# Attention mask as extra features, output weights cast later, channel sum on VectorE, three products moved forward

## The chip, the cores and the metric

The kernel runs on one core of a Trainium2 chip. The metric is the device time of one execution in microseconds (us). A difference of about 0.2% (3.6 us) is what a measurement of this kernel can tell from none.

## The reference

Two layers of a Conformer block on 512 tokens of width 1024. Each layer is a half-weighted SwiGLU, a mixing stage, a second half-weighted SwiGLU and a norm. The mixing stage, where the change lies, is this:

```python
h = rms_norm(x, mix_norm);  p = h @ w_in
# group A: 8 heads, q and k of 96 features (64 + 32 rotary), v of 64
scores = q @ k.T * 96 ** -0.5                  # keys up to the end of the 128-row query tile
allowed = k_chunk <= q_chunk                   # chunks of 64 tokens
scores = where(allowed, scores, -1e30)
attn = softmax(scores) @ v
# group B: conv module on 512 channels
u = a * sigmoid(g)
y = causal_depthwise_conv(u, 31 taps) + conv_b
conv = silu(layer_norm(y, ln_g, ln_b))         # mean and variance over the 512 channels
x = x + concat(attn, conv) @ w_out
```

## The kernel before

Activations lie as features (128 partitions) by tokens (512 columns). Every large product in float32 precision is done as three float32r products (`mm3`, lines 151 to 155): high by high, high by low, low by high. A weight block of 128x1024 is loaded by SP, cast to the high part on ScalarE (ACT, line 136), and its low part is made either by a subtraction on VectorE (DVE) or GpSimd (POOL) (line 142), or, for the kind "sum", by ACT writing the negated block (line 139) and a POOL-queued DMA that adds the weight to it in memory (line 140). The pools hold 3 raw blocks, 4 high and 4 low parts.

The program is written in order, and a scheduler sets the order of each engine's queue; `issue_after(i)` keeps what stands in it behind instruction i in that order. Each engine then works its own queue in order.

The mixing stage (`mix_body`) first makes the projections, the queries `q` and keys `kn` (tokens by heads by 96 features). Then, for eight heads, with a lag of some steps between them: `turn` transposes a head's queries and keys (TensorE, PE, lines 765 and 770; evicted by ACT at 767 and DVE at 772); `scores` makes four score blocks of 128, 256, 384 and 512 keys (788), adds the mask with a small bf16 product into the last 64 columns of each (789: a row of ones for the first 64 queries by a row of -1e30), takes the maximum on DVE (790) and the exponential with its row sum on ACT (794); `turn_p` transposes the probabilities (809, evicted by DVE, ACT, DVE at 812); `values` multiplies by v (822) and, for each pair of heads, normalises on DVE (829); `turn_out` transposes the result of a pair (840) and splits it into high and low parts (159, 160), which gives one of the four blocks `at`.

The depthwise convolution runs beside this. Channel blocks 0 and 3 are done on DVE (876), each ended by a copy on ACT (886). Blocks 1 and 2 are done by ACT and POOL together: per tap, ACT writes the scaled shifted input `pr` (880, three buffers) and POOL adds it (884). The last 15 adds of block 1 and all 30 of block 2 are held behind the last inverse norm of the keys.

After that comes the layer norm over channels: POOL sums the four blocks (898 to 900), PE spreads the mean with a matrix of 1/512 (902), DVE subtracts it (908), ACT squares and DVE adds (185, 189), PE sums over channels (196), POOL takes the inverse root (171), PE spreads it (215), DVE scales (918), ACT applies SiLU (920), and the split gives the four blocks `cv`. The output projection multiplies eight blocks of output weights `wo` by `at` and `cv`. The products with `at` of the first weight blocks fill PE while the layer norm's chain runs; they stand behind the last score product. The first four `wo` blocks are loaded and cast as soon as the keys are done (line 866), with kind "sum"; the others come late, with the subtraction on POOL.

## Time and profile before

| | us |
|---|---|
| median of 3 runs | 1815.6 |
| lowest, highest | 1813.96, 1816.92 |
| the profiled execution, its own time | 1814.81 |
| span of its profile, first to last instruction | 1813.0 |
| idle time of PE within the span (1813.0 - 1791.5) | 21.5 |
| first to last exponential, layer 0 | 463.4 to 508.1 |
| first to last exponential, layer 1 | 1356.0 to 1400.7 |

The profile gives, for each engine, the time it was busy and what it waited for; a row of the timeline has the start, the length, the engine, the line, the operation, out<-in, and in brackets the idle time before it with what ended it. Rows of the same kind that follow each other are merged (xN), and then the length runs from the first start to the last end. The length of a row includes the end of an instruction that overlaps the next one's start, so the distance between starts is what one more instruction costs. A float32 product shows two records for each instruction.

### The profile page before, as it was taken

The page shows a single profiled execution, that of the slowest core. Times are in us where ns is not written, and L with a number is a line of the kernel's source. Part 1 is how long each engine was busy: PE and PEld are TensorE (multiplying, and loading weights), DVE is VectorE, ACT ScalarE, POOL GpSimd, SP SyncE. Part 2 cuts the span into 40 slices and gives each one's busy share as a digit, 9 for nine tenths or more (in the row PEclk, how much of TensorE's full clock was granted, in tenths as well). Part 3 has the DMA queues.
Part 4 walks back from the last instruction along what each step waited for, and adds up shares of the span by engine and source line. Part 5 has one row for each costly group of instructions (what it writes and reads, how often), then busy time and mean ns, then how long its engine had stood idle before and what let it go on. Part 6 is the DMA issues. An engine that isn't in the chain of part 4 may idle for free.

```text
span 1813.0 us, 30598 instructions
## 1 busy us (share of the span) xinstructions
PE 1791.5 (99%) x12198; PEld 1649.3 (91%) x12198; DVE 1423.0 (78%) x1975; ACT 1089.3 (60%) x1685; POOL 422.7 (23%) x343
## 2 busy tenths in 40 slices
PE   9899999999999999999999999999999999999998
PEld 7799999888788899999888999998978788999997
DVE  5988887679965978887679888865999568888873
ACT  4565656447953565656645656564679435656564
POOL 1000000238944001010220000002589420000001
PEclk9999999999999999999999999999999999999999
DMA  5466665323203456565325575743250125565642
GB/s 177 115 166 159 156 158 129 127 76 113 63 1 112 121 154 166 150 165 141 111 76 160 126 189 126 189 117 110 80 143 9 36 87 157 142 183 132 183 115 73
DMA packets 70415, 226.23 MB, mean 125 GB/s; under 512 B 7936, under 2 KB 8320, under 8 KB 70272
## 3 DMA queue, kind: packets, MB, share of 16 engines
q1 hardware_dynamic: 54000, 169.74, 27.8%
q0 software_dynamic: 16128, 54.53, 17.5%
q8 instruction: 95, 1.56, 0.3%
q14 instruction: 48, 0.39, 0.1%
q10 hardware_dynamic: 144, 0.00, 0.0%
HBM read 222.15 MB, written 2.10 MB: 124 GB/s over the span
## 4 chain that ended last, share of the span: by engine, by line
PE 80%; DVE 9%; ACT 5%; POOL 3%; issue 2%; DMA 0%; ACTq 0%; POOLq 0%; DVEq 0%
PE ps L154 25%; PE ps L152 25%; PE ps L153 25%; POOL y L884 2%; PE ps L822 1%; ACT pr L880 1%; DVE wl L244 1%; DVE r L160 1%; DVE x L449 1%; ACT r L794 1%; PE ps L788 1%; DVE cv L876 1%; DVE wl L142 1%; DVE r L311 1%; PE ps L196 0%
## 5 line engine op out<-in xcount | busy, mean ns | idle before, releaser
L152 PE MATMUL ps<-r,wh 128*128 128x256 f32 (+1 forms) x3436 | 1062.3, 312 | 5.7 <-ACT r L159 5.0
L153 PE MATMUL ps<-r,wh 128*128 128x256 f32 (+1 forms) x3436 | 1063.9, 310 | 0.0
L154 PE MATMUL ps<-r,wl 128*128 128x256 f32 (+1 forms) x2668 | 846.8, 319 | 2.2 <-DVE wl L142 0.8
L152 PEld LDWEIGHTS ps<-r,wh 128*128 128x128 f32 x3436 | 652.1, 190 | 45.4 <-ACT r L159 6.7
L153 PEld LDWEIGHTS ps<-r,wh 128*128 128x128 f32 x3436 | 653.6, 190 | 36.6 <-issue 2.4
L154 PEld LDWEIGHTS ps<-r,wl 128*128 128x128 f32 x2668 | 507.7, 190 | 40.4 <-DVE wl L244 2.6
L136 ACT CAST wh<-raw 128x1024 fp32r<-128x1024 f32 (+3 forms) x148 | 132.1, 900 | 221.1 <-PE ps L153 102.8
L367 POOL DMA_DIRECT2D ls<-in_wgu x72 | 62.7, 871 | 744.3 <-ACT ls L366 617.6
L142 DVE TENSOR_TENSOR wl<-raw,wh 128x1024 fp32r<-128x1024 f32 (+3 forms) x132 | 146.4, 1115 | 100.1 <-ACT wh L136 93.2
L242 ACT CAST wh<-fr 128x1024 fp32r<-128x1024 f32 (+1 forms) x160 | 157.6, 985 | 101.2 <-DVE fr L387 43.5
L154 PE MATMUL ps<-r,ls 128*128 128x256 f32 x768 | 216.7, 282 | 0.0
L244 DVE TENSOR_TENSOR wl<-fr,wh 128x1024 fp32r<-128x1024 f32 (+1 forms) x160 | 182.3, 1139 | 39.5 <-ACT wh L242 39.5
L884 POOL TENSOR_TENSOR y<-y,pr 128x511 f32<-128x511 f32 (+14 forms) x120 | 157.6, 1314 | 54.6 <-ACT pr L880 47.3
L154 PEld LDWEIGHTS ps<-r,ls 128*128 128x128 f32 x768 | 145.2, 189 | 0.0
L244 DVE TENSOR_TENSOR wl<-raw,wh 128x1024 fp32r<-128x1024 f32 (+1 forms) x100 | 113.3, 1133 | 24.7 <-ACT wh L242 24.2
L189 POOL TENSOR_TENSOR r<-r,t 128x512 f32<-128x512 f32 x45 | 77.4, 1729 | 172.6 <-ACT t L185 171.8
L242 ACT CAST wh<-raw 128x1024 fp32r<-128x1024 f32 (+1 forms) x100 | 97.9, 979 | 27.9 <-PE ps L153 20.0
L366 ACT ACTIVATE ls<-fr 128x1024 fp32r<-128x1024 f32 (+1 forms) x56 | 56.1, 1002 | 78.6 <-PE ps L154 66.6
L880 ACT ACTIVATE pr<-r,vec 128x511 f32<-128x511 f32 (+14 forms) x120 | 85.5, 737 | 10.2 <-POOL y L884 10.2
L876 DVE SCALAR_TENSOR_TENSOR cv<-r,vec,cv 128x511 f32<-128x511 f32 (+14 forms) x120 | 87.7, 731 | 3.4 <-ACT cv L872 2.1
L449 DVE SCALAR_TENSOR_TENSOR x<-ps,x 128x512 f32<-128x512 f32 x112 | 77.0, 688 | 16.5 <-PE ps L154 16.1
L367 POOL DMA_DIRECT2D ls<-in_wdq x32 | 27.7, 865 | 260.1 <-ACT ls L366 260.1
(220 smaller groups left out, 2439.0 us busy)
## 6 DMA issues: line engine op xcount, KB each, us to landing
fr<-in_wgu SPq DMA_DIRECT2D x112, 512.0 KB, 3.7
ls<-in_wgu POOLq DMA_DIRECT2D x72, 512.0 KB, 6.4
raw<-in_wgu SPq DMA_DIRECT2D x62, 512.0 KB, 5.1
fr<-in_wdq SPq DMA_DIRECT2D x48, 384.0 KB, 4.6
ls<-in_wdq POOLq DMA_DIRECT2D x32, 384.0 KB, 4.7
raw<-in_wd SPq DMA_DIRECT2D x32, 384.0 KB, 3.1
raw<-in_wd SPq DMA_DIRECT2D x32, 256.0 KB, 2.7
raw<-in_wcv SPq DMA_DIRECT2D x16, 512.0 KB, 3.2
```

The lines of the kernel that those rows point to most:

```text
L136: order["cast"] = A.copy(hi[:, :w], raw[:, :w]).ins
L142: (G if kind in POOLW.split() else V).tensor_tensor(lo[:, :w], raw[:, :w], hi[:, :w].bitcast(FP), ALU.subtract)
L152: T.matmul(o, lh, rh, start=first, stop=False, skip_group_check=free)
L153: T.matmul(o, lh, rl, start=False, stop=False, skip_group_check=free)
L154: order["mm"] = T.matmul(o, ll, rh, start=False, stop=last, skip_group_check=free).ins
L242: A.copy(hi[:, :w], src[:, :w])
L244: order["lo"] = V.tensor_tensor(lo[:, :w], src[:, :w], hi[:, :w].bitcast(FP), ALU.subtract).ins
L367: G.dma_start(out=lo[:, :n], in_=w, accum_op=ALU.add)
L449: return V.scalar_tensor_tensor(v, o.rearrange("p (m t) -> p m t", m=2), 0.5 * sign, v, ALU.mult, ALU.add).ins
L876: V.scalar_tensor_tensor(acc[:, s:], u[c][:, :S - s], tap(k), acc[:, s:], ALU.mult, ALU.add)
L880: A.activation(pr[:, s:], u[c][:, :S - s], AF.Copy, scale=tap(k))
L884: order["conv"] = G.tensor_tensor(acc[:, s:], acc[:, s:], pr[:, s:], ALU.add).ins
```

## The change

- Mask: `q` and `kn` get 100 columns per head, not 96. Column 96+t of a query is 1 for the first 64 tokens of token tile t, and of a key is -1e30 for the last 64 tokens of tile t. They come from the constants (32 columns more) by two POOL products per layer (`mask_columns`). Transposes, evictions and score products take 100 rows; the 64 mask products (32 per layer) and their constants are gone.
- Output weights: only three blocks are loaded with kind "sum", and each is put behind the last exponential of head 0, 2 and 4. The fourth is now of the kind with the subtraction on POOL.
- Products: the nine products of the first output block with the first three blocks of `at` are put right behind the last `values`, ahead of the last `turn_out`.
- Channel sum: three adds on DVE in place of three on POOL, with the last POOL block added last; the mean's matrix is all ones, and the scale -1/512 moves into the subtraction on DVE.

```diff
+DM = DQ + 4
-EARLY = "s"
+WOH = (0, 2, 4)
-WOP = 4
-CN = 256
+CCOS, CSIN, CID, CMQ, CMK = 0, 64, 128, 256, 272
+CN = 288
...
-        q = kpool.tile([P, NT, H, DQ], FP, tag="q", name=nm("q"), bufs=1)
-        kn = kpool.tile([P, NT, H, DQ], FP, tag="kn", name=nm("kn"), bufs=1)
+        q = kpool.tile([P, NT, H, DM], FP, tag="q", name=nm("q"), bufs=1)
+        kn = kpool.tile([P, NT, H, DM], FP, tag="kn", name=nm("kn"), bufs=1)
...
+        def mask_columns(v, o):
+            G.tensor_tensor(v[:, :, :, DQ:DM], cst[:, o:o + 16].rearrange("p (t i) -> p t i", t=NT)[:, :, None, :]
+                            .to_broadcast([P, NT, H, 4]), ones.rearrange("p (t h i) -> p t h i", t=NT, h=H), ALU.mult)
...
-                T.matmul(o, qT[0:DQ, i * P:(i + 1) * P], kT[0:DQ, 0:n], start=True, stop=False)
-                heads[h]["s"] = T.matmul(o[:, n - 64:n], mrow, mneg, start=False, stop=True).ins
+                heads[h]["s"] = T.matmul(o, qT[0:DM, i * P:(i + 1) * P], kT[0:DM, 0:n], start=True, stop=True).ins
...
+        wo, early = [], []
+        def early_products(ms, ks):
+            for m in ms:
+                if m == len(early):
+                    early.append(bank())
+                group(early[m], wo[m], at, ks, KD)
         for step in range(H + 6):
             for stage, lag in STAGES:
                 h = step - lag
+                if stage is turn_out and h == H - 1:
+                    for m, i in enumerate(WOH):
+                        with tc.issue_after(order["keys"]), tc.issue_after(heads[i]["e"]):
+                            wo.append(load_w(wout[l, m], WC, "sum"))
+                    with tc.issue_after(order["values"]):
+                        early_products((0,), range(3))
...
-        with tc.issue_after(order["keys"]):
-            wo = [load_w(wout[l, m], WC, "sum") for m in range(WOP)]
...
+        with tc.issue_after(heads[H - 1]["s"]):
+            early_products((0,), range(3, 4))
         ysum = tmp()
-        G.tensor_tensor(ysum, ys[0], ys[1], ALU.add)
-        G.tensor_tensor(ysum, ysum, ys[2], ALU.add)
-        (G if YP else V).tensor_tensor(ysum, ysum, ys[3], ALU.add)
+        for a, b in ((ys[0], ys[1]), (ysum, ys[3]), (ysum, ys[2])):
+            V.tensor_tensor(ysum, a, b, ALU.add)
         pm = bank()
-        T.matmul(pm, onesm, ysum, start=True, stop=True)
+        T.matmul(pm, ones, ysum, start=True, stop=True)
...
-            V.tensor_tensor(ys[c], ys[c], pm, ALU.subtract)
+            V.scalar_tensor_tensor(ys[c], pm, -1.0 / CW, ys[c], ALU.mult, ALU.add)
...
+    consts[:64, CMQ:CMQ + 16] = np.eye(NT, dtype=f32).reshape(-1)
+    consts[64:, CMK:CMK + 16] = f32(-1e30) * np.eye(NT, dtype=f32).reshape(-1)
```

How the queues move. First ACT's queue in layer 0 from the first exponential of head 0 (r,sums is the exponential with its row sum, pr a conv tap, wh and wl the two parts of an output weight block). Before, the fourth weight block stands just ahead of it:

```order
L880 ACTIVATE pr_5573<-r_4161,vec 128x488
L880 ACTIVATE pr_5576<-r_4161,vec 128x487
L139 ACTIVATE wl_5467<-raw_5463 128x1024
L136 CAST wh_5465<-raw_5463 128x1024
L880 ACTIVATE pr_5579<-r_4161,vec 128x486
L794 ACTIVATE r_4887,sums_4885<-ps_4882,mx_4886 128x128
L880 ACTIVATE pr_5582<-r_4161,vec 128x485
```

In the change (the exponential is at line 787 there, the tap at 885, the cast at 123 and the negated copy at 126) taps stand ahead of it, and the first weight block comes behind the last exponential of head 0:

```order
L885 ACTIVATE pr_5550<-r_4153,vec 128x484
L885 ACTIVATE pr_5553<-r_4153,vec 128x483
L787 ACTIVATE r_4881,sums_4879<-ps_4876,mx_4880 128x128
L787 ACTIVATE r_4882,sums_4879<-ps_4877,mx_4880 128x384
L885 ACTIVATE pr_5556<-r_4153,vec 128x482
L787 ACTIVATE r_4883,sums_4879<-ps_4878,mx_4880 128x512
L761 ACTIVATE r_4901<-ps_4896,gqs_4802 100x512
L123 CAST wh_5397<-raw_5395 128x1024
L787 ACTIVATE r_4914,sums_4879<-ps_4910,mx_4913 128x128
L126 ACTIVATE wl_5399<-raw_5395 128x1024
```

So three weight blocks that stood ahead of the first exponential in the queue, and the fourth just ahead of it, now stand between exponentials. From the first exponential to the last (the 256-wide one of head 7) ACT's queue has 79 rows before in either layer: 32 exponentials, 32 taps, 15 evictions and copies. In the change it has 85 in layer 0 and 83 in layer 1: 31 and 29 taps, and 7 rows of output weights.

The third and the fourth block, further on in ACT's queue of the change, stand behind the last exponential of head 4 (to `sums_5062`) and ahead of the eviction of transposed probabilities (line 805):

```order
L885 ACTIVATE pr_5605<-r_4730,vec 128x496
L787 ACTIVATE r_5066,sums_5062<-ps_5061,mx_5063 128x512
L123 CAST wh_5411<-raw_5409 128x1024
L126 ACTIVATE wl_5413<-raw_5409 128x1024
L123 CAST wh_5844<-raw_5842 128x1024
L805 COPY r_5087<-ps_5086 128x512
L885 ACTIVATE pr_5608<-r_4730,vec 128x495
```

No such rows stand there before; there the eviction follows the exponential.

Last, the end of the attention stage on PE (layer 0). Before, the last transposes (840) and the mean's product (902) follow the last values (822):

```order
L822 MATMUL ps_5399<-r_4880,r_5388 128x64
L840 MATMUL ps_5433<-cst,t_5431 128x128 x4
L902 MATMUL ps_5722<-t_5718,onesm 128x512
L152 MATMUL ps_5726<-r_5210,wh_5444 128x512
L153 MATMUL ps_5726<-r_5211,wh_5444 128x512
L154 MATMUL ps_5726<-r_5210,wl_5446 128x512
```

In the change nine products with weights (139 to 141) stand between:

```order
L815 MATMUL ps_5361<-r_4874,r_5350 128x64
L139 MATMUL ps_5416<-r_5180,wh_5397 128x512
L140 MATMUL ps_5416<-r_5181,wh_5397 128x512
L141 MATMUL ps_5416<-r_5180,wl_5399 128x512
L139 MATMUL ps_5416<-r_5305,wh_5397 128x512
L140 MATMUL ps_5416<-r_5306,wh_5397 128x512
L141 MATMUL ps_5416<-r_5305,wl_5399 128x512
L139 MATMUL ps_5416<-r_5377,wh_5397 128x512
L140 MATMUL ps_5416<-r_5378,wh_5397 128x512
L141 MATMUL ps_5416<-r_5377,wl_5399 128x512
L833 MATMUL ps_5426<-cst,t_5393 128x128 x4
L899 MATMUL ps_5690<-t_5686,ones 128x512
```

Between the mean's product and the product that sums the squares stand 24 products of this kind before and 15 in the change; further on the counts are the same. On DVE the three adds of the channel sum stand behind the normalisation of the last pair of heads (829), ahead of the last split.

## The prediction

> **What bounds the kernel now.** I read the page's busy times first:

> ```profile
> span 1813.0 us, 30598 instructions
> ...
> PE 1791.5 (99%) x12198; PEld 1649.3 (91%) x12198; DVE 1423.0 (78%) x1975; ACT 1089.3 (60%) x1685; POOL 422.7 (23%) x343
> ```

> PE looks like the bound everywhere, ACT nowhere. But the change lies in one stage per layer, so the windows come next, split at the first score product and the last exponentials (columns: the stretch, its length, then busy time and count of PE, PEld, DVE, ACT, POOL, granted clock, DMA):

> ```profile
> core 0: us, PE busy (x) PEld busy (x) DVE busy (x) ACT busy (x) POOL busy (x), PEclk, DMA share, GB/s
> 447.00:458.50 11.50, 11.50 (x60) 9.55 (x58) 9.20 (x12) 9.16 (x14) 11.19 (x11) 1.00 0.84 199
> 458.50:510.00 51.50, 49.15 (x348) 39.13 (x348) 47.96 (x94) 50.28 (x122) 46.44 (x39) 1.00 0.13 28
> 1340.00:1356.00 16.00, 15.26 (x81) 12.21 (x80) 15.64 (x19) 13.91 (x20) 14.26 (x14) 1.00 0.74 166
> 1356.00:1401.00 45.00, 44.12 (x316) 35.30 (x314) 42.77 (x85) 43.95 (x113) 40.76 (x34) 1.00 0.11 25
> ```

> In the attention stretch ACT is busy 50.28 of 51.50 us in layer 0 and 43.95 of 45.00 in layer 1: it has 1.2 and 1.05 us left, less than PE. Ahead of the stretch it has 2.3 and 2.1 us left, and that is where the output weights are cast now. The view of waits says what PE lacks:

> ```profile
> PE ps L788 <- ACT r L794: 1.9, 3, 1.1
> ```

> Little, in both layers together: PE and ACT are both full, and neither waits much for the other. ACT's timeline, first and last exponential of either layer:

> ```profile
> 459.73 1.29 ACT L880 ACTIVATE pr<-r,vec 128x488 f32<-128x488 f32 x2
> 460.92 1.06 ACT L139 ACTIVATE wl<-raw 128x1024 fp32r<-128x1024 f32 x1
> 461.87 1.04 ACT L136 CAST wh<-raw 128x1024 fp32r<-128x1024 f32 x1
> 462.80 0.70 ACT L880 ACTIVATE pr<-r,vec 128x486 f32<-128x486 f32 x1
> 463.40 0.36 ACT L794 ACTIVATE r<-ps,mx 128x128 f32<-128x128 f32 x1
> ...
> 507.53 0.52 ACT L794 ACTIVATE r<-ps,mx 128x256 f32<-128x256 f32 x1
> ...
> 1356.00 0.35 ACT L794 ACTIVATE r<-ps,mx 128x128 f32<-128x128 f32 x1
> ...
> 1400.16 0.52 ACT L794 ACTIVATE r<-ps,mx 128x256 f32<-128x256 f32 x1
> ```

> By the distance of starts a tap costs 0.60 ((460.92 - 459.73) / 2) and a weight row 0.95 (460.92 to 461.87). From first start to last end ACT takes 44.65 us in either layer (508.05 - 463.40; 1400.68 - 1356.00).

> **Output weights cast later.** ACT's queue between those two exponentials gains 7 weight rows and loses 1 tap in layer 0, 3 in layer 1: 7 x 0.95 = 6.65, less 0.60 or 1.80, is +6.05 and +4.85 us, into stretches with 1.2 and 1.05 us to spare. This is the term that decides. Two things give some of it back. (a) The first exponential can start earlier, as no cast stands before it. But a tap needs its buffer back from the third add before, and POOL's adds are slow at that place:

> ```profile
> 447.20 0.89 POOL L140 DMA_DIRECT2D wl<-in_wout  x1
> ...
> 449.68 5.91 POOL L884 TENSOR_TENSOR y<-y,pr 128x495 f32<-128x495 f32 x4
> ...
> 1339.99 0.92 POOL L140 DMA_DIRECT2D wl<-in_wout  x1
> ...
> 1354.64 0.27 DVE L790 TENSOR_REDUCE mx<-ps 128x1 f32<-128x128 f32 x1
> ```

> Without the weight DMA the adds start at 447.20. An add takes up to 1.48 here (5.91 / 4); I take 1.38 as the mean of the stretch. The last tap ahead of the exponential in the change (483 columns) needs the buffer of the tap with 486, the 11th add: 447.2 + 11 x 1.38 = 462.4, and with the tap itself the exponential starts at 463.0, 0.4 earlier. In layer 1 nine adds are needed: 1340.0 + 9 x 1.38 = 1352.4; there the first maximum on DVE (1354.64 before) comes later than that, and I take 1354.3 for the exponential, 1.7 earlier. At best (adds of 1.25, maxima in time) it is 2.0 and 2.6. (b) Of the 44.65 us the rows' own costs explain 43.7, so some 0.9 was waiting; I take 0.4 of it as saved, since PE is no longer what ACT waits for; bounds 0.9 saved and 2 lost. Last exponential: 6.05 - 0.4 - 0.4 = +5.25 in layer 0 (508.05 to 513.3), 4.85 - 1.7 - 0.4 = +2.75 in layer 1 (1400.68 to 1403.4).

> **From the last exponential to the layer norm.** Behind it on PE stand the transposes of head 7, the values of head 6, a transpose and the values of head 7:

> ```profile
> 509.53 1.26 PE L809 MATMUL ps<-cst,r 128*128 128x128 f32 x10
> 510.63 2.34 PE L822 MATMUL ps<-r,r 128*128 128x64 f32 x20
> ...
> 513.25 2.34 PE L822 MATMUL ps<-r,r 128*128 128x64 f32 x20
> 516.38 0.66 PE L840 MATMUL ps<-cst,t 128*128 128x128 f32 x4 [0.79 <-DVE t L829]
> 516.87 1.02 PE L902 MATMUL ps<-t,onesm 128*128 128x512 f32 x2
> ```

> Before, PE came to them 1.5 us after the exponential's end (509.53 against 508.05): its own backlog. That cushion is the first to go. Then the order itself costs 3.72 to the start of the last values (509.53 to 513.25) and 3.13 more until they are normalised and PE can turn them (516.38). On DVE the three sum adds now stand behind that normalisation; three adds of this size in a row took 2.28 (the first row of the next fence). With 0.15 for the hand-over from ACT: 0.15 + 3.72 + 3.13 + 2.28 = 9.3 us from the last exponential to the mean's product. PE itself, with nine products at 0.23 and four transposes, is there at 8.6, so it waits 0.7 for the sum. Before it was 8.82 in layer 0 (516.87 - 508.05) and 9.27 in layer 1. So the forward products fill the 0.79 us wait and still do not bring the mean forward. POOL's conv is no bound: its last add ends some 1.3 us behind the last tap, and that stands one row ahead of the last exponential in layer 0 and some 3 us behind it in layer 1.

> **The chain behind the mean.**

> ```profile
> 520.69 2.28 DVE L189 TENSOR_TENSOR r<-r,t 128x512 f32<-128x512 f32 x3
> ...
> 522.99 0.39 PE L154 MATMUL ps<-r,wl 128*128 128x512 f32 x1
> 523.22 0.95 PE L196 MATMUL ps<-ones,r 128*128 128x1 f32 x8
> ...
> 525.51 0.69 DVE L211 TENSOR_TENSOR t<-cst,rtok 128x512 f32<-128x512 f32 x1 [1.15 <-POOL rtok L171]
> ...
> 526.88 1.02 PE L215 MATMUL ps<-t,ones 128*128 128x512 f32 x2
> ...
> 530.80 1.21 PE L152 MATMUL ps<-r,wh 128*128 128x512 f32 x4 [0.17 <-ACT r L159]
> ...
> 1409.95 2.08 PE L902 MATMUL ps<-t,onesm 128*128 128x512 f32 x2 [0.41 <-POOL t L900]
> ...
> 1425.61 1.19 PE L152 MATMUL ps<-r,wh 128*128 128x512 f32 x4 [0.17 <-ACT r L159]
> ```

> From the mean to the first product with `cv` it is 13.93 us in layer 0 and 15.66 in layer 1. The chain itself needs 13.0: in layer 0 about 0.9 of the 13.9 is PE finishing fill products (the adds ended at 522.97 and PE came at 523.22; the spread's input ended at 526.20 and PE came at 526.88). With nine products fewer behind the mean (9 x 0.23 = 2.05 us, 0.23 from 522.99 to 523.22) PE now waits for the chain, so I take 13.0 in both. First `cv` product: layer 0 513.3 + 9.3 + 13.0 = 535.6 against 530.80, +4.8; layer 1 1403.4 + 22.3 = 1425.7 against 1425.61, +0.1. What stands behind it is unchanged.

> **The mask.**

> ```profile
> 481.74 1.10 PE L788 MATMUL ps<-r,r 96*128 96x512 f32 x2
> 482.68 0.19 PE L789 MATMUL ps<-mneg,mrow 128*128 128x64 bf16 x1
> 482.71 1.97 PE L822 MATMUL ps<-r,r 128*128 128x64 f32 x16
> ...
> L788 PE MATMUL ps<-r,r 96*128 96x384 f32 (+3 forms) x128 | 45.2, 465 | 2.2 <-ACT r L794 1.9
> ```

> [...] It is removed from PE inside the stretches where ACT now sets the pace: worth 0 here, 3.2 if that cover is gone. The mask columns go on POOL in an idle stretch before the stage. What four rows more in the contraction cost no row shows: 0 at least, 4/96 of the scores' 45.2 us, 1.9, at most. [...] The new subtraction replaces one of the same width: 0.

> **Sum.** +4.8 + 0.1 = +4.9 on the profiled execution's 1814.81: 1819.7. That execution lies 0.8 under the median of the runs (1815.6), so 1820.5 for a median. Own range: (a) at its best gives back 1.6 and 0.9, (b) at its best 0.5 in each layer, at its worst it adds 2.4 in each: +1.4 to +9.7, 1817 to 1825.3.

> **The rivals.** *PE sets the pace after all* (faster). If ACT's rows were not what holds the end, the stage would lose the masks (3.2) and PE's waits for exponentials (1.9), and the chain would start without the POOL wait: the nine products (2.05) take the place of the 0.79 wait and of 0.9 of fill in layer 0, +0.3, and in layer 1 of the 2.7 that its chain is over 13.0, -1.4. Together -6.2: 1809.4. For it: PE is busy 49.15 of the 51.50 us too, and came to the last transposes 1.5 us after ACT had done its part. Against: ACT's rows from the first to the last exponential now add up to 49.8 us in layer 0, and PE's whole stretch from the first score to the last transposes was 51, 49 without waits, 47.4 without masks, started 4.5 us earlier. It needs some 5 us of ACT's queue per layer to cost nothing. 0.14.

> *The cast blocks stall the conv pair too* (slower still). Two or three weight rows in a run, 1.9 to 2.85 us, leave POOL without taps, and a POOL subtraction stands among its adds:

> ```profile
> L142 POOL TENSOR_TENSOR wl<-raw,wh 128x1024 fp32r<-128x1024 f32 x8 | 21.8, 2746 | 30.4 <-PE ps L153 30.4
> ```

> 2.7 us each. With three buffers ACT then waits for POOL: if each of the three blocks loses 0.7, a layer loses 2 more: 1824.5. Three buffers of 1.3 us cover about 2.6, which speaks against more. 0.18.

> *Nothing measurable*: the mechanism of the forecast with (a) and (b) at their best, 1817. It is in the forecast's own 0.63, of which 0.25 lies within 0.2%.

> *The clock drops* in PE's new gaps. With PE idle 2.35 of 51.50 us the granted clock was 1.00, as in every window above. If it halved for the 6 us from the transposes (509.53) to the end of the last values (near 515.5) in both layers, that is +12: 1832.5. 0.03. [...]

> *The four rows cost PE time*, so that the mask does not gain what it says: +1.9 at most, 1822.4. 0.02.

> **The numbers.** Bound for faster or slower: 3.6 us (0.2%). Faster 0.14 (PE pace). Within: 0.25 of the forecast's case and 0.01: 0.26. Slower: 0.38 of the forecast, 0.18, 0.03, 0.01: 0.60. Predicted 1820.5. The range 1812.5 to 1826 leaves out the first rival but for its slow edge, the clock and the worst stalls, some 0.2.

> **What would show it.** ACT busy over 98% from the first to the last exponential, that stretch near 49.5 us in layer 0 and 48.5 in layer 1 where it was 44.65. PE waits for exponentials of 8 us or more in place of 1.9, most of all ahead of the last transposes of probabilities. The mean's product about 9.3 us behind the last exponential, and PE waiting for the sum of squares. No wait for POOL at the mean. If the stretch stays under 46 us, or PE shows no new wait for ACT, the forecast is wrong.

## The result, and the profile after

The changed kernel is slower: 1826.62 us as the median of four executions (1824.06 to 1827.9), beside 1814.78 for the kernel before (four, 1813.01 to 1816.92). The ratio is 1.0063, 95% interval 1.0046 to 1.0080, so +11.8 us. The prediction had the sign and +4.9; its range ended at 1826, just under the median. The forecast's cause, rows added to a full ACT queue, is borne out below, so the sign is not luck; the size was missed. The profiled execution took 1827.9 us, 13.1 more than the profiled one before.

First the head of the page of the changed kernel, then the windows that answer to those of before (stretch, its length, busy time and count of PE, PEld, DVE, ACT, POOL, granted clock, DMA share, GB/s), cut at the first and last exponential of either layer:

```profile
span 1826.1 us, 30455 instructions
...
PE 1795.2 (98%) x12134; PEld 1649.8 (90%) x12134; DVE 1424.1 (78%) x1976; ACT 1089.0 (60%) x1683; POOL 421.4 (23%) x341
```

```profile
core 0: us, PE busy (x) PEld busy (x) DVE busy (x) ACT busy (x) POOL busy (x), PEclk, DMA share, GB/s
458.50:463.00 4.50, 3.81 (x19) 2.20 (x17) 4.26 (x8) 3.23 (x6) 4.19 (x5) 1.00 0.00 0
463.00:514.00 51.00, 44.85 (x282) 34.67 (x282) 42.64 (x83) 50.14 (x119) 45.08 (x37) 0.97 0.31 73
...
1361.50:1413.00 51.50, 46.96 (x291) 38.34 (x288) 44.44 (x86) 49.42 (x116) 43.22 (x36) 0.90 0.30 72
```

ACT is busy 50.14 of 51.00 us and 49.42 of 51.50; PE is idle 6.15 and 4.54 us in stretches where it was idle 2.35 of 51.50 and 0.88 of 45.00 before. And the clock is under 1.00. What PE waited for in the whole run (total, times, longest), and ACT's first and last exponential of either layer:

```profile
PE ps L782 <- ACT r L787: 5.4, 5, 1.5
...
PE ps L183 <- DVE r L176: 2.8, 2, 1.4
PE ps L802 <- DVE r L805: 1.4, 1, 1.4
PE ps L815 <- DVE r L805: 1.2, 1, 1.2
...
PE ps L899 <- DVE t L897: 0.8, 2, 0.4
```

```profile
463.19 0.35 ACT L787 ACTIVATE r<-ps,mx 128x128 f32<-128x128 f32 x1
...
513.12 0.59 ACT L787 ACTIVATE r<-ps,mx 128x256 f32<-128x256 f32 x1
...
1361.67 0.37 ACT L787 ACTIVATE r<-ps,mx 128x128 f32<-128x128 f32 x1 [0.27 <-DVE mx L783]
...
1412.12 0.48 ACT L787 ACTIVATE r<-ps,mx 128x256 f32<-128x256 f32 x1
```

The exponentials take 50.52 us in layer 0 (463.19 to 513.71) and 50.93 in layer 1, where both took 44.7. The two waits for DVE's evictions (L805) are both in layer 1, 2.6 of the 4.54 us that PE is idle there; why DVE comes late at these two places was not tried. PE's last wait in the stretch of layer 0, and what stands behind the exponentials on PE (L802 transposes of probabilities, L815 values, L833 transposes of a head pair, L899 the mean, L183 the sums of squares, L202 the spread):

```profile
496.14 0.44 PE L802 MATMUL ps<-cst,r 128*128 128x128 f32 x2 [0.53 <-ACT r L761]
496.59 2.44 PE L815 MATMUL ps<-r,r 128*128 128x64 f32 x20
...
515.22 1.26 PE L802 MATMUL ps<-cst,r 128*128 128x128 f32 x10
...
518.93 2.34 PE L815 MATMUL ps<-r,r 128*128 128x64 f32 x20
523.25 0.60 PE L833 MATMUL ps<-cst,t 128*128 128x128 f32 x4
524.27 1.10 PE L899 MATMUL ps<-t,ones 128*128 128x512 f32 x2 [0.43 <-DVE t L897]
530.23 1.02 PE L183 MATMUL ps<-ones,r 128*128 128x1 f32 x8 [1.45 <-DVE r L176]
533.97 1.02 PE L202 MATMUL ps<-t,ones 128*128 128x512 f32 x2
...
1423.72 1.10 PE L899 MATMUL ps<-t,ones 128*128 128x512 f32 x2 [0.41 <-DVE t L897]
...
1434.92 1.02 PE L202 MATMUL ps<-t,ones 128*128 128x512 f32 x2
```

The spread came at 526.88 and 1421.69 before: layer 0 gives 7.1 us away, layer 1 another 6.1. The clock, last, in windows cut where it changes:

```profile
485.76:489.17 3.41, 2.16 (x16) 1.74 (x16) 3.41 (x9) 2.61 (x8) 3.17 (x4) 1.00 0.01 2
489.17:492.58 3.41, 3.41 (x18) 3.15 (x17) 3.41 (x8) 3.36 (x8) 3.25 (x3) 0.50 0.03 7
1366.40:1369.81 3.41, 1.95 (x6) 0.99 (x7) 3.41 (x7) 3.41 (x10) 3.07 (x4) 1.00 0.46 144
1369.81:1373.22 3.41, 3.41 (x14) 2.83 (x13) 3.41 (x7) 3.41 (x10) 2.39 (x3) 0.50 0.69 126
1376.64:1380.05 3.41, 2.02 (x20) 1.79 (x17) 3.38 (x7) 3.41 (x9) 2.45 (x3) 1.00 0.52 159
1380.05:1386.88 6.83, 6.83 (x28) 5.88 (x28) 4.48 (x8) 6.13 (x15) 6.03 (x6) 0.50 0.46 77
1427.84:1431.25 3.41, 2.05 (x13) 1.57 (x12) 1.64 (x4) 0.16 (x1) 0.34 (x1) 1.00 0.00 0
1431.25:1434.66 3.41, 3.41 (x9) 2.64 (x8) 0.69 (x1) 0.00 (x0) 0.70 (x1) 0.50 0.00 0
```

Four times PE is idle 1.25 to 1.46 us within 3.41 us, and the next 3.41 us, or twice that, run at half clock. In the two stages that is 17 us at half; the kernel before has one such stretch of 3.4 us, behind the mean of layer 1.

### The profile page after: what moved, and what is told of

The parts are those of the page before. It is cut to its first block, busy times and chain, and to the rows that moved or that the text cites. A ratio compares the mean times of both kernels' runs of the same rounds, so it can differ in the third digit from the quotient of the medians.

```text
span 1826.1 us, 30455 instructions
## 1 busy us (share of the span) xinstructions
PE 1795.2 (98%) x12134; PEld 1649.8 (90%) x12134; DVE 1424.1 (78%) x1976; ACT 1089.0 (60%) x1683; POOL 421.4 (23%) x341
## 4 chain that ended last, share of the span: by engine, by line
PE 79%; DVE 10%; ACT 4%; POOL 4%; issue 2%; DMA 0%; SPq 0%; ACTq 0%; POOLq 0%; DVEq 0%
PE ps L141 25%; PE ps L139 25%; PE ps L140 24%; POOL y L889 2%; PE ps L815 2%; DVE wl L231 1%; DVE cv L881 1%; DVE r L147 1%; PE ps L782 1%; DVE x L436 1%; POOL sck L158 1%; ACT pr L885 1%; PE ps L802 1%; DVE wl L129 1%; PE ps L183 1%
## 5 line engine op out<-in xcount | busy, mean ns | idle before, releaser
L139 PE MATMUL ps<-r,wh 128*128 128x256 f32 (+1 forms) x3436 | 1061.8, 312 | 6.1 <-ACT r L146 4.6
L140 PE MATMUL ps<-r,wh 128*128 128x256 f32 (+1 forms) x3436 | 1063.7, 310 | 0.1
L139 PEld LDWEIGHTS ps<-r,wh 128*128 128x128 f32 x3436 | 651.5, 190 | 46.6 <-ACT r L146 6.6
L140 PEld LDWEIGHTS ps<-r,wh 128*128 128x128 f32 x3436 | 653.0, 190 | 36.9 <-issue 2.2
L436 DVE SCALAR_TENSOR_TENSOR x<-ps,x 128x512 f32<-128x512 f32 x112 | 77.1, 689 | 13.7 <-PE ps L141 13.4
```

The lines of the kernel that those rows point to most:

```text
L139: T.matmul(o, lh, rh, start=first, stop=False, skip_group_check=free)
L140: T.matmul(o, lh, rl, start=False, stop=False, skip_group_check=free)
L436: return V.scalar_tensor_tensor(v, o.rearrange("p (m t) -> p m t", m=2), 0.5 * sign, v, ALU.mult, ALU.add).ins
```

## The experiments

Three theories stand in the expectations. **Q**: the late casts overload ACT's queue and PE pays for it. **C**: the order behind the last exponential (sum on DVE, forward products) costs 2 to 3 us a layer. **K**: PE's waits lower the clock, and that adds. Each ratio is to the kernel before, run between the executions of the experiment.

**1. Casts put back (e1).**

```diff
-for m, i in enumerate(WOH):
-    with tc.issue_after(order["keys"]), tc.issue_after(heads[i]["e"]):
-        wo.append(load_w(wout[l, m], WC, "sum"))
+with tc.issue_after(order["keys"]):
+    wo += [load_w(wout[l, m], WC, "sum") for m in range(4)]
```

> The changed kernel with the output weights loaded and cast where the kernel before does it (four of them, ahead of the attention stretch); mask columns, channel sum on DVE and forward products stay. Theory Q (the late casts overload ACT's queue, about +5 us of rows a layer, and the lower clock comes from PE's waits for it): the last exponentials end within 1.5 us of where they ended before (508.05 and 1400.68), no granted clock under 0.95 between the exponentials, time 1810 to 1816, so 11 to 16 us under the changed kernel's 1826.6. Rival C (the order behind the last exponential, DVE sum and forward products, costs 2 to 3 us a layer by itself): 1818 to 1821.

Measured: 1815.01 against 1813.47, ratio 1.0007 (0.9998 to 1.0016). Its windows:

```profile
463.00:506.00 43.00, 40.88 (x276) 32.85 (x277) 41.60 (x81) 42.81 (x111) 38.92 (x32) 1.00 0.12 26
...
1356.00:1399.00 43.00, 41.71 (x278) 32.94 (x277) 42.09 (x83) 42.80 (x111) 38.88 (x32) 1.00 0.11 25
```

The exponentials end at 506.0 and 1399.0, 2.1 and 1.7 us earlier than before. Over the kernel before, the changed kernel is 11.8 us slower and this one 1.5: 10.3 us are gone with this one part. Q holds, C is out as the main cause.

**2. Late casts alone (e2).**

```diff
-with tc.issue_after(order["keys"]):
-    wo = [load_w(wout[l, m], WC, "sum") for m in range(WOP)]
+for m, i in enumerate((0, 2, 4)):
+    with tc.issue_after(order["keys"]), tc.issue_after(heads[i]["e"]):
+        wo.append(load_w(wout[l, m], WC, "sum"))
```

> The kernel before with one part of the change: three output weights cast behind the exponentials of heads 0, 2 and 4 in place of four ahead of the attention. Mask products, channel sum on POOL and the order of the output products stay. Theory Q: this part makes the whole loss or more, since the mask products stay on PE: 1824 to 1830, ACT over 98% busy between the exponentials, PE waits for exponentials of 5 us or more, a granted clock under 0.95 in some windows of 4 us. Rival C: only +4 to +6, 1819 to 1821.

Measured: 1824.03 against 1813.47, ratio 1.006 (1.0046 to 1.0074), +10.6. The windows between its exponentials:

```profile
463.00:512.00 49.00, 43.03 (x297) 33.44 (x298) 42.51 (x83) 48.84 (x117) 43.42 (x36) 1.00 0.31 76
1359.40:1410.60 51.20, 45.77 (x309) 35.84 (x308) 43.65 (x84) 50.05 (x118) 45.07 (x38) 0.97 0.30 73
```

ACT is full, PE idle 6.0 and 5.4 us, and the stretches are 4 and 6 us longer. The clock is 1.00 in layer 0 all the same: the loss does not need the half clock.

**3. The change without forward products (e3)**: the twelve products of each group stand behind the mean as in the kernel before.

```diff
-    with tc.issue_after(order["values"]):
-        early_products((0,), range(3))
...
+        early_groups(range(0, 2))
```

> The changed kernel with the first output products where the kernel before has them (behind the mean and the statistics); late casts, mask columns and the channel sum on DVE stay. The prediction gave the forward products no gain and no cost: 1825 to 1828. Theory Q says the same. Rival C: they stand ahead of the mean's product and behind them PE waits for DVE, so without them 2 to 4 us less: 1822.5 to 1824.5. If they filled a wait that now opens again: 1828 to 1830.

**4. Mask columns and sum on DVE, all else as before (e4).** The diff is the change's own for the mask, and

```diff
-        G.tensor_tensor(ysum, ys[0], ys[1], ALU.add)
...
+        for a, b in ((ys[0], ys[1]), (ysum, ys[3]), (ysum, ys[2])):
+            V.tensor_tensor(ysum, a, b, ALU.add)
```

> The kernel before with two parts of the change: mask columns in place of mask products, and the channel sum on DVE. Casts ahead of the attention and the output products as before. The prediction's sizes: masks 0 to 3.2 us saved (all of it if PE paces the stretch once ACT's queue is as before), the sum on DVE 0 to -1: 1810.5 to 1815. Rival: ACT's queue paces the stretch in the kernel before too, so masks gain nothing and DVE's three adds cost what POOL's did: 1814 to 1816.

Measured: e3 1833.41, ratio 1.011 (1.0096 to 1.0124); e4 1817.92, ratio 1.0022 (1.0014 to 1.0031). Both miss. Late casts cost 15.5 us between these two, and the forward products, to which the prediction gave nothing, are worth 8.1 us with late casts (e3 is 19.9 us over the kernel before, the changed kernel 11.8) and 2.9 with early ones (1817.9 to 1815.0). The rows say why; the mean of e4's layer 0, and its windows around it:

```profile
516.51 2.04 PE L894 MATMUL ps<-t,ones 128*128 128x512 f32 x2 [2.09 <-DVE t L892]
```

```profile
512.82:516.23 3.41, 0.82 (x6) 0.44 (x5) 3.14 (x5) 1.76 (x2) 0.00 (x0) 1.00 0.00 0
516.23:519.64 3.41, 3.13 (x6) 1.83 (x7) 1.18 (x3) 0.64 (x3) 0.00 (x0) 0.50 0.00 0
```

Without the nine products PE has nothing between the values and the sum: it waits 0.78 for the normalised values and 2.09 for DVE's adds, and the clock halves within that wait in both layers. In e3 the same wait of 2.09 stands ahead of the mean in both layers, with 3.4 and 6.8 us at half clock that start just behind it or within it. So the products fill not only the 0.79 us of before but the hole that the sum on DVE opens. What they do for the clock is less sure: e4's two stages have 13.7 us at half and e1's 6.8, but e3 and the changed kernel have 17.1 each.

**5. Forward products alone (e5)**, on the kernel before (sum on POOL, mask products).

```diff
+                if stage is turn_out and h == H - 1:
...
+                    with tc.issue_after(order["values"]):
+                        early_products((0,), range(3))
...
+        with tc.issue_after(heads[H - 1]["s"]):
+            early_products((0,), range(3, 4))
```

> The kernel before with one part of the change: the nine products of the first output group ahead of the last values' transposes, one with head pair 7's data behind them, twelve behind the mean, twelve behind the sums. Mask products, channel sum on POOL, early casts stay. The prediction gave this part 0 or +0.3 in layer 0: 1813 to 1815. Theory K (a stretch of 3.41 us with 1.0 us or more of PE idle can be followed by a stretch at half clock, each 1.7 us of PE work lost): the idle 1.19 us ahead of the mean in layer 1, behind which the kernel before lost 1.7, is filled; a new wait of about 1.4 us for the sum of squares opens behind the mean, as in the first experiment, in both layers. 1811.5 to 1813.5 if neither new wait drops the clock, 1815 to 1817 if both do.

**6. Mask columns alone (e6)**; the mean is a product with ones, scaled in the subtraction.

```diff
-T.matmul(o, qT[0:DQ, i * P:(i + 1) * P], kT[0:DQ, 0:n], start=True, stop=False)
-heads[h]["s"] = T.matmul(o[:, n - 64:n], mrow, mneg, start=False, stop=True).ins
+heads[h]["s"] = T.matmul(o, qT[0:DM, i * P:(i + 1) * P], kT[0:DM, 0:n], start=True, stop=True).ins
```

> The kernel before with one part of the change: mask columns in place of the 64 mask products (the mean is a product with ones, scaled in the subtraction, which costs the same). Channel sum on POOL, early casts and output products as before. The prediction: 0 to -3.2. By the first experiments the exponentials' stretch shrinks from 44.7 to 43.0 us a layer; if the end followed, 1810 to 1811. Theory K: what PE saves it spends waiting for POOL's sum ahead of the mean (about 1.8 us more idle), the mean comes some 0.5 to 1 us earlier at most, and the clock halves behind the idle time in one or both layers: 1813 to 1818.

Measured: e5 1822.54 against 1813.58, ratio 1.0043 (1.003 to 1.0057); e6 1814.34, ratio 1.0004 (0.9995 to 1.0012). The mask by itself changes nothing that can be measured; the exponentials end 1.3 and 1.6 us earlier, and the mean hardly moves (516.52 and 1410.09, where it was 516.87 and 1409.95), since it waits 0.45 and 1.75 us for POOL's sum. With e4, the sum on DVE, added to the mask columns, costs some 3.6 us. e5 is the surprise: +9.0 and no late cast in it. Its PE queue at the mean of layer 0 (L840 transposes, L152 and L153 products with the last head pair, L906 the mean):

```profile
519.00 0.60 PE L840 MATMUL ps<-cst,t 128*128 128x128 f32 x4
520.28 0.49 PE L152 MATMUL ps<-r,wh 128*128 128x512 f32 x1 [0.68 <-ACT r L159]
521.00 0.50 PE L153 MATMUL ps<-r,wh 128*128 128x512 f32 x1 [0.23 <-DVE r L160]
...
521.57 1.02 PE L906 MATMUL ps<-t,onesm 128*128 128x512 f32 x2
```

The three products with the last head pair were put ahead of the mean; they wait for that pair's split, and the mean stands behind them in the queue, 4.7 us later than before.

**7. Late casts taken apart (e7)**: the second row of each weight is held back to the next head.

```diff
-wo.append(load_w(wout[l, m], WC, "sum"))
+wo.append(load_w(wout[l, m], WC, "sum", heads[i + 1]["e"]))
```

> The changed kernel with the same seven weight rows on ACT inside the attention stretch, but each pair of cast and negated copy taken apart by about a head, so that no two stand together but the last. The queue's sum is the same. Theory Q (ACT's queue sets the end): 1825 to 1828, last exponential less than 1 us from the changed kernel's place. Theory K (runs of casts make PE's gaps and the half clock behind them adds to the loss): fewer windows at half clock in the attention stretches (there are 3 of them, 5.1 us, in layer 1 and 1 in layer 0 in the changed kernel), 1820 to 1824.

Measured: 1828.84, ratio 1.0078 (1.0066 to 1.0091), above both ranges. The two attention stretches have 6.8 us at half clock where the changed kernel has 13.7, and the time is not less: K is not the main cause, and the same rows cost no less when they stand apart. The exponentials of layer 0 end at 512.18, 1.5 us earlier than in the changed kernel, but the mean comes only 0.3 earlier (523.97), so the end does not follow ACT's last exponential. The spread comes at 535.24, 1.3 later, behind 3.4 us at half clock that the changed kernel does not have there.

**8. The fill shared out anew (e8)**, with early casts: six more products ahead of the sums of squares, six of a fourth group ahead of the spread.

```diff
         early_products((1,), range(4))
+        early_products((2,), range(2))
...
-        early_products((2,), range(4))
+        early_products((2,), range(2, 4))
+        early_products((3,), range(2))
```

> Early casts, mask columns, channel sum on DVE and forward products, and the fill behind the mean shared out anew: eighteen products ahead of the sum of squares in place of twelve, then twelve (six of them of a fourth group) ahead of the spread. Theory K: PE's wait of 1.43 to 1.45 us for the sum of squares shrinks to 0.1 or less, the half clock behind it (6.8 us long in layer 1 of the first experiment, 3.4 us of work) does not come, and PE's idle time in both layers falls by some 2.8: 1809 to 1812.5, under the kernel before. Rival (the chain behind the mean sets the end, so fill is worth nothing): 1814 to 1816.

Measured: 1817.24, ratio 1.0015 (1.0007 to 1.0024), 2.2 us more than e1 and above both ranges. PE no longer waits for the sums, but it has used up its fill: behind the spread of either layer it waits 2.9 us for `cv`, and the clock halves at its end.

```profile
527.76:531.17 3.41, 1.12 (x4) 0.24 (x2) 1.88 (x3) 1.47 (x3) 0.00 (x0) 1.00 0.00 0
531.17:538.00 6.83, 6.22 (x15) 4.86 (x16) 3.28 (x5) 3.53 (x7) 0.00 (x0) 0.50 0.00 1
```

A hole was moved, not closed. The chain itself must get shorter.

**9. The mean earlier (e9)**, with early casts: the convolution and the sum are written ahead of the last values, and the mean ahead of the nine products.

```diff
+            if step == H + 3:
...
+                for a, b in ((ys[0], ys[3]), (ysum, ys[1]), (ysum, ys[2])):
+                    V.tensor_tensor(ysum, a, b, ALU.add)
...
+                    with tc.issue_after(order["values"]):
+                        T.matmul(pm, ones, ysum, start=True, stop=True)
                         early_products((0,), range(3))
...
-        early_products((1,), range(4))
+        early_products((1,), range(3))
+        early_products((0, 1), range(3, 4))
```

> Early casts, mask columns, channel sum on DVE and forward products, with the convolution and the sum written ahead of the last values, so that DVE adds before it normalises head pair 7, and the mean's product stands ahead of the nine products in place of behind the last transposes; the pair 7 products stand behind nine of the next group. If the chain behind the last POOL add (511.8 us in layer 0 of the first experiment, mean at 516.84) is what opens PE's waits of 0.41 and 1.43 us, the mean comes near 513.9, PE does not wait for the sum of squares, no clock under 0.95 behind it: 1808 to 1811.5, under the kernel before by 2 to 5. Rival (the chain sets nothing, PE's work does): 1814 to 1815.5.

Measured: 1810.68 against 1813.67, ratio 0.9982 (0.9973 to 0.9991). It is the one version that beats both kernels, 3 us under the kernel before and 15 under the changed one. The 3 us are a little less than the 3.6 named at the start, but the interval leaves out 1. Mean, sums and spread of layer 0:

```profile
513.56 1.08 PE L892 MATMUL ps<-t,ones 128*128 128x512 f32 x2
...
521.15 1.02 PE L183 MATMUL ps<-ones,r 128*128 128x1 f32 x8 [0.58 <-DVE r L176]
524.87 1.02 PE L202 MATMUL ps<-t,ones 128*128 128x512 f32 x2
```

The mean of layer 0 stands at the end of the values with no wait (in layer 1 it waits 0.79), the wait for the sums is 0.58 in place of 1.45, and neither stage has a window at half clock.

**10. Late casts behind the exponentials (e10)**: e3 with the six rows behind ACT's last copy of probabilities.

```diff
+with tc.issue_after(order["keys"]):
+    raws = [load_raw(wout[l, m], WC) for m in range(3)]
-with tc.issue_after(order["keys"]), tc.issue_after(heads[i]["e"]):
-    wo.append(load_w(wout[l, m], WC, "sum"))
+with tc.issue_after(heads[H - 1]["c"]):
+    wo.append(load_w(wout[l, m], WC, "sum", raws[m]))
```

> The third experiment's kernel (late casts, mask columns, sum on DVE, output products behind the mean) with the six late weight rows moved again: behind ACT's last copy of probabilities, where ACT was idle for some 2 to 4 us at a time. The raw weights are loaded early. Theory Q (it is ACT's full queue between the exponentials, not lateness as such): the exponentials' stretch returns to 43 us, time 1817 to 1822, against 1833.4 with the casts between the exponentials and 1817.9 with them ahead. Rival (casts after the start of the attention cost wherever they stand, through their DMA or POOL): 1826 to 1833.

Measured: 1823.22 against 1813.67, ratio 1.0049 (1.0036 to 1.0061): 10 us under e3, so it is the place between the exponentials that costs. The raw loads and the weights' DMA moved with the rows and were not tried apart; against them as the cause speaks that ACT did not stand waiting in the changed kernel's stretch (busy 50.14 of 51.00 us). The exponentials' stretch is 43.3 and 43.8 us again. It ends a little over the range expected. The rows of layer 0 show what it pays instead: PE waits for the sum, then for the weights' low part, and in each layer 10.2 us at half clock start within the first of these waits.

```profile
517.78 2.05 PE L904 MATMUL ps<-t,ones 128*128 128x512 f32 x2 [1.96 <-DVE t L902]
...
521.58 0.80 PE L145 MATMUL ps<-r,wl 128*128 128x512 f32 x1 [0.90 <-DMA wl<-in_wout]
```

**11. One late load (e11).**

```diff
-with tc.issue_after(order["keys"]), tc.issue_after(heads[i]["e"]):
+with tc.issue_after(order["keys"]), tc.issue_after(heads[i]["e"]) if m == 2 else nullcontext():
```

> The changed kernel with one late load in place of three (weights 0 and 1 as before, weight 2 behind head 4's exponentials, weight 3 as in the changed kernel): three late rows on ACT in place of seven, 2.85 us in place of 6.65. ACT had about 1.2 us to spare in either layer. Queue alone, straight in the rows: 1815 + 3/7 of 11.6 = 1820. With the slack used up first: 1815 + 2 x (2.85 - 1.2) = 1818.3. If the loss comes from PE's long waits behind runs of casts and the half clock: one run of three is left per layer, 1817 to 1819.

Measured: 1820.63, ratio 1.0042 (1.0029 to 1.0054), 5.4 us over e1 for three rows where seven cost 10.3. The loss goes with the rows from the first one on; the 1.2 us that ACT seemed to have left bought nothing that shows.

**12. Forward products with the mean ahead of the last pair (e12).**

```diff
-        with tc.issue_after(heads[H - 1]["s"]):
-            early_products((0,), range(3, 4))
...
+        order["mean"] = T.matmul(pm, onesm, ysum, start=True, stop=True).ins
...
+        with tc.issue_after(order["mean"]):
+            early_products((0,), range(3, 4))
```

> The fifth experiment's kernel (the kernel before with forward products alone) with the three products of head pair 7 behind the mean's product and not ahead of it. In the fifth experiment PE waited 0.68 and 0.23 us for the split of that pair ahead of the mean, and the mean came 4.7 us later than before. If that order was its loss: the mean near 519.5 or before (transposes at 519.0 in layer 0 there), time 1814 to 1817. If the nine products themselves push the mean back (9 x 0.23 = 2.07 a layer): 1818 to 1820.

Measured: 1816.53, ratio 1.0012 (1.0004 to 1.0021), mean at 517.40. So 6 of e5's 9 us were three products in the wrong place in a queue, with the 10.2 us at half clock that e5's stages have and e12's have not; the time is in the first of the two ranges.

**13 to 15. The changed kernel three times more (e13, e14, e15)**, to see the same instructions with the half clock at other places.

> The changed kernel once more, as it is, for a second profile of it. Every drop of the clock so far starts at a multiple of 3.413 us from the others of the same profile, at a place that differs from profile to profile. Theory K: the drops fall behind other waits this time, the clock time lost differs, and the span follows it: more lost, longer span, by about 0.7 to 1 us for 1 us. If the half clock cost nothing (work that would wait anyway), the span would not follow.

> The changed kernel a third time, with the same question: between 0 and 10 us of PE work lost to half clock in the two stages, span 1819 to 1829 with it.

> The changed kernel a fourth time, with the same question. A profile with no drop in either stage would show what ACT's queue costs by itself: by the changed kernel's profile 13.1 - 6.9 + 1.7, some 8 us over the kernel before without its own drop.

Measured: spans of 1827.6, 1822.8 and 1828.9 us, beside 1826.1 in the first profile. The windows from the first transposes of queries to the last addition to `x`, two layers each: first the kernel before, then the changed kernel's first profile, then e14, then e15.

```profile
451.29:565.03 113.74, 110.20 (x649) 89.39 (x648) 87.56 (x141) 83.83 (x170) 81.55 (x60) 1.00 0.21 58
1344.73:1459.83 115.10, 111.88 (x649) 90.35 (x648) 90.20 (x142) 83.97 (x170) 81.35 (x59) 0.99 0.20 56
```

```profile
450.83:572.12 121.29, 112.16 (x617) 88.94 (x616) 90.06 (x143) 86.86 (x173) 80.58 (x58) 0.99 0.21 58
1352.39:1473.06 120.67, 113.99 (x617) 93.06 (x616) 89.30 (x143) 86.88 (x172) 79.84 (x57) 0.94 0.21 58
```

```profile
450.77:572.10 121.33, 112.31 (x617) 88.58 (x616) 90.15 (x143) 86.86 (x173) 80.59 (x58) 0.99 0.21 58
1352.08:1469.73 117.65, 110.47 (x617) 89.14 (x616) 89.63 (x144) 86.29 (x172) 79.75 (x57) 0.99 0.22 59
```

```profile
451.56:574.50 122.94, 115.90 (x617) 92.88 (x616) 90.24 (x143) 87.05 (x173) 80.70 (x58) 0.94 0.21 57
1355.22:1475.85 120.63, 113.97 (x617) 93.01 (x616) 89.74 (x144) 86.86 (x172) 79.79 (x57) 0.94 0.21 58
```

The two stages of the changed kernel take 238.98, 241.96, 243.18 and 243.57 us (e14, the first profile, e13, e15) with 6.8, 17.1, 27.3 and 27.3 us at half clock in them. That is 0.2 to 0.3 us for each us at half, an estimate from these four executions, so a stretch of 3.4 costs 0.7 to 1.0, and not the 1.7 of work that it takes from PE (products of 512 columns start 0.43 us apart in the stretch at 1431.25, 0.23 outside): the rest falls into time that PE would have waited. Taken off at that price, the changed kernel's stages take about 237.3 and those before (228.84 with 3.4 us at half) about 228.0. So of the 13.1 us between the two profiles some 9 are waits and 3 to 4 the clock. The windows above say the same another way: from the first pair to the second PE is idle 9.1 us more (6.76 to 15.81) and busy 4.1 us more. The 8 us expected without a drop are near that. For each us of PE work lost the stages grow by 0.4 to 0.6, where 0.7 to 1 was expected, and none of the four executions was free of drops.

**16. e9 with late casts (e16).**

```diff
-with tc.issue_after(order["keys"]):
-    wo += [load_w(wout[l, m], WC, "sum") for m in range(4)]
+for m, i in enumerate(WOH):
+    with tc.issue_after(order["keys"]), tc.issue_after(heads[i]["e"]):
+        wo.append(load_w(wout[l, m], WC, "sum"))
```

> The ninth experiment's kernel with the changed kernel's late casts (behind heads 0, 2 and 4) in place of early ones. Theory Q with the end set by PE: late casts cost what they cost with the other orders behind the last exponential (10.3 to 15.5 us), 1820 to 1824. If a part of that loss came only from how the last transposes, the sum and the products were queued, less than 8 us: under 1818.5.

Measured: 1824.31 against 1814.26, ratio 1.0058 (1.0044 to 1.0071), 13 us over e9 by the two differences and just above the first range. With four orders behind the last exponential, late casts cost 10.6 (e2), 15.5 (e4 to e3), 10.3 (e1 to the change) and 13 us. The loss arises in the attention and none of these orders behind it wins it back. Against the changed kernel e16's earlier mean gains 1.8 us, less than can be told from none, where e9's gained 4.5 over e1.

## Why the prediction came out too low

**ACT's full queue.** Right, and shown: 10.3 of the 11.8 us go with the casts (e1), they cost as much alone (e2), and moving them behind the exponentials takes 10 us off (e10). The sum of rows put the last exponential of layer 0 at 513.3; it ended at 513.71. Against the end of layer 0's stage, the first exponential of layer 1 is 1.4 us earlier, where 1.7 was forecast, and the last 4.8 later, where 2.75 was; in e14, with less half clock, 3.1. One of the forecast's own signs failed: PE's waits for exponentials came to 5.4 us and not to 8 or more, and none stood ahead of the last transposes.

**"That cushion is the first to go."** This is the step that failed. The prediction let PE arrive at the last transposes with ACT's last exponential and counted 9.3 us from there to the mean. PE arrived 1.51 us behind it in layer 0 (515.22 against 513.71), as before (1.5), and 2.06 in layer 1 (1.4 before), and the mean came 10.6 and 11.1 us behind. In layer 0 PE's waits stood between 461 and 496; from 496.6 to the mean's wait at 523.8 it was busy without a gap, working off what stood in its queue. So the end is not ACT's last exponential plus a chain. It is PE's work plus what PE had to wait before. This is why e7's exponentials, 1.5 us earlier, brought the mean only 0.3 forward. The 1.5 us were not a store that waits could use up: in e7 PE waited 1.36 us for an exponential as late as 505.88 and was still 2.73 behind at the last transposes. The step cost 1.3 and 1.8 us. No row shows the 0.15 for the hand-over from ACT that is in the 9.3: where PE waited for an exponential in the attention stages of either kernel, it went on 0.05 us behind the end of ACT's row.

**The chain of 13.0 us.** 9.70 us from mean to spread in layer 0, with 3.92 more to the first `cv` product (as before, 526.88 to 530.80): 13.6. PE did wait for the sums, 1.45 us, as forecast. But the prediction also took off the 0.68 us by which PE came late to the spread, and the twelve products ahead of the spread are as many as before: its input ended at 533.28 and PE came at 533.97. Mis-sized by 0.6 a layer; in layer 1 the half clock behind that wait makes it 15.1 (13.5 in e14, which has none there).

**Layer 1 at +0.1.** It gave 6.1 away. In e14, with 3.4 us at half clock in it as before, its stage still takes 2.6 us more than before, by the steps above; the rest is the clock.

**The clock at 0.03.** This is the other step that failed, a term that the sum put at nothing. The rival happened, though not at its place or size: it was put at the last transposes and came behind waits in the middle of the attention and at the sums. By the three repeats it costs 3 to 4 of the 13.1 us of the profiled pair. Waits of 1.52 us and less were enough in the changed kernel's profile. And the prediction read no half clock in its own rows, where one stands: the mean of layer 1 (1409.95, 2.08 us long against 1.02 in layer 0) is within 3.4 us at a granted clock of 0.50 that start at 1409.97, behind a stretch with 1.19 us of idle time.

**The tally.** The profiled pair differs by 13.1 us where 4.9 was forecast. Of the 8.2 us between, the cushion makes 3.1, the chain 1.2 and ACT's stretches 0.7 (for layer 1 the last two are read from e14). The remaining 3.2 are put down to the clock, in line with the 3 to 4 above.

**The mask worth 0** is borne out where it stands alone (e6, ratio 1.0004), though the cover is POOL's sum and not ACT there. No run shows the 3.2 us at which the prediction has the masks: from a block of 512 keys to the next instruction behind it and its mask it is 0.97 us before, and 0.86 for the block of 100 rows in the change (medians of 16). Over the four widths that makes 4.6 us for the 64 masks, an estimate from such medians, and e6's time shows none of it. Whether the columns gain or lose beside late casts was not tried by itself. **Forward products worth 0** was wrong: they gain 2.9 to 8.1 us where the sum is on DVE (e3, e4), by the hole they fill, and lose 2.9 where it is on POOL (e12; 0.7 to 3.8 by its interval). **The sum on DVE** was counted in the chain as three adds, 2.28 us; what it costs beyond that, without the forward products (e4), is PE's wait of 2.09 us and the clock; with them the wait is 0.43. The stall of the conv pair (0.18) came as PE waits of another kind: ACT waited for POOL 1.4 us in all in layer 0, less than the rival's price.

## What to carry to other kernels

Before moving work to a later place, look whether the engine has slack *in that stretch*; if it is full there, expect to pay about the whole length of the moved rows (10.9 us by the forecast's rows, 10.3 to 15.5 measured), in the waits of whoever it feeds. Where two engines are both full, count the loss on the one whose work sets the end, as work plus waits, and not as a chain from the other's last instruction. And in an in-order queue ask of each forward-moved instruction what it waits for: three products with unready data ahead of a mean cost 6 us (e5 to e12, the clock included), and the same mean put ahead of work that was ready gained 4.5 (e1 to e9).

## What the hardware showed

The same kernel's time goes with it: of the 72 executions of the kernel before that were timed beside the experiments, the 28 with a mean clock of 0.998 took 1813.3 us on average, the four with 0.995 took 1816.4.
